# Output product with two of eight pairs of K tiles as seven block products

## The chip, the cores and the metric

The kernel runs on one core of a Trainium2 chip. A core has five engines that run side by side, each its own list of instructions in a fixed order: TensorE (PE in the profile, its weight loads PEld), VectorE (DVE), ScalarE (ACT), GpSimd (POOL) and SyncE (SP, which here issues the transfers). They meet through semaphores. The metric is the device time of one execution in microseconds, lower is better; the time before is the median of three runs.

## The reference

One layer on x of 256 rows by 2048 columns: a SwiGLU feed-forward half step, a mixing step of two head groups with one input projection and one output projection, a second feed-forward half step and a norm. What the change touches is the output projection, the second line here:

```python
y = concatenate([y_rwkv, y_lru], axis=-1)      # 256 x 2048
h = h + y @ w_out[l]                           # w_out: 2048 x 2048
h = h + 0.5 * swiglu(rms_norm(h, ffn2_norm[l]), ...)
```

`y_rwkv` (columns 0 to 1023 of y) comes from a recurrence, `y_lru` (columns 1024 to 2047) from a second recurrence whose result is normed over its 1024 columns: `y_lru = rms_norm(scan * gelu(gate), lru_norm)`.

## The kernel before

All matrix products are made at about float32 precision from two rounded parts of each operand, `hi` and `lo` (`hi` is the operand cast to fp32r, `lo` what is left): a product is three matmuls, hi by hi, hi by lo and lo by hi, that add up in one PSUM bank of 128 by 512.

**The output product** is `mix_out`. It makes two passes (`hf`), one for each half of 1024 columns of w_out. In a pass K runs over 16 tiles of 128 (`NK`), and the 256 rows are two tiles (`t`), the 1024 columns two blocks of 512 (`n`): four banks, each with 3 matmuls for each K tile, so 12 matmuls for a K tile and 192 for a pass. The first pass adds up in banks 0 to 3, the second in banks 4 to 7. Behind each pass DVE adds the banks into `h` (L1099), and `half_done` transposes this half of `h` for the next norm (`transposed`, L228 on PE, L236 on ACT, L237 on DVE), in banks 0 to 3 behind the first pass and 4 to 7 behind the second. K tiles 0 to 7 are `y_rwkv` (tile `xahi_887`, `xalo_888` in the orders below), K tiles 8 to 15 are `y_lru` (`xahi_1042`, `xalo_1043`); both are split by `split_rows` (L1019 on ACT, L1020 on DVE) at the end of `mix_layer`, and the last of these stand while the first pass already runs.

**The weights** come through `weights`: one transfer of 1 MB for two K tiles into `wst` (three buffers), then for each K tile a cast `whi` on ACT (L96) and a difference `wlo` on DVE (L97), 128 by 1024, three buffers each. A transfer starts when the buffer it writes has been split; a cast starts when the matmuls of the K tile three before are through.

**The other scheme is already in the kernel**, in both feed-forward parts: `rows_times_pairs`, with a plan such as `nSnSnSnn`. It takes K tiles in pairs. A pair `n` is 24 matmuls as above. A pair `S` is a 2 by 2 block product by the scheme of Strassen and Winograd: seven products of 128 by 512 instead of eight, 21 matmuls. For it DVE makes four differences of the weight blocks (L136 to L138, in a second buffer of `wst`, called t1 to t4), and these are split as well (three splits of 1024 and one of 512, the last through a tile `whb` of one buffer). The rows need four block sums too, in hi and lo (`block_sums`: four adds of 128 by 128, one cast and one difference of 512). Three of the seven products are shared between outputs: they add up in four banks `aux` beside the four banks `own`, over all S pairs of a pass, and behind the last S pair `shared_h` adds them into `h`.

What sets the order: the program is written in the order of the source, and a scheduler orders each engine's list by priorities and its own estimates when the program is built. On the chip each list then runs in that order.

```python
                self.three(own[0], x(1, 0), w["b21"], first, last)
                self.three(aux[0], x(0, 0), w["b11"], f, l)
                self.three(own[1], sm(4), w["b22"], first, last)
```

In these lines of `rows_times_pairs`, `x` is a block of the rows, `sm` a block sum, and the first three of a pair's seven products are seen.

## Time and profile before

| what | us |
|---|---|
| median of three runs | 1919.07 (1916.38 to 1921.64) |
| the profiled execution, its own time | 1916.57 |
| its span in the trace | 1914.8 |
| PE busy | 1880.0 (98%) |
| DVE busy | 1577.2 (82%) |
| ACT busy | 1033.6 (54%) |
| the output product, first matmul to last | about 1097.3 to 1194.4 |

The span is the time in the trace from the first to the last instruction; 1.8 us of the execution lie around it. A busy engine is one that has an instruction in flight: a matmul of 512 columns is listed with some 390 ns, but the next one starts 227 ns after it. So PE's rate is read from starts, and its idle time from rows that carry a bracket `[idle before <-releaser]`.

### The profile page before, as it was taken

The numbers are of one execution on the slowest core, as the hardware profiler recorded it, in microseconds if no ns is written. First come the engines' busy times: TensorE is split into PE (matmuls) and PEld (weight loads), VectorE is DVE, ScalarE is ACT, GpSimd is POOL, SyncE is SP. The second block draws the span as 40 slices with busy tenths as digits, with TensorE's granted clock in tenths as the row PEclk, the third lists the DMA queues.
The fourth block names the chain that finished last, engine by engine and source line by source line (L and its number), as shares of the span: only waits on it lengthen the run. The fifth ranks groups of instructions, "written<-read, shape, count | busy, mean of one in ns | idle before, by whom it ended". The sixth has DMA issues, their size and how long they took to land.

```text
span 1914.8 us, 25801 instructions
## 1 busy us (share of the span) xinstructions
PE 1880.0 (98%) x10161; PEld 1584.8 (83%) x10161; DVE 1577.2 (82%) x2044; ACT 1033.6 (54%) x1261; POOL 9.7 (1%) x53
## 2 busy tenths in 40 slices
PE   7999999999999999999999999999999999999997
PEld 6888888888888889898899978888888888788886
DVE  7889889898978776976595775989898988987876
ACT  6555555555555555543454554655555555564553
POOL 0000000000000001000000000000000000000000
PEclk9999999999999999998999999999999999999999
DMA  7565555655656556545243456555655655756664
GB/s 238 165 209 180 189 206 184 211 182 207 229 199 228 208 198 212 180 122 152 78 147 116 129 200 204 187 205 184 211 185 204 221 182 176 259 188 203 214 205 141
DMA packets 124402, 360.78 MB, mean 188 GB/s; under 512 B 20879, under 2 KB 23128, under 8 KB 124152
## 3 DMA queue, kind: packets, MB, share of 16 engines
q1 hardware_dynamic: 123960, 358.08, 55.7%
q8 instruction: 79, 1.29, 0.3%
q10 hardware_dynamic: 320, 1.06, 0.1%
q14 instruction: 43, 0.35, 0.1%
HBM read 351.25 MB, written 7.86 MB: 188 GB/s over the span
## 4 chain that ended last, share of the span: by engine, by line
PE 70%; DVE 15%; DMA 11%; issue 2%; ACT 2%; DVEq 0%; SPq 0%; ACTq 0%
PE bank L150 16%; PE bank L149 16%; PE bank L151 16%; DMA wst<-in_ffn_w_gate_dram 6%; DVE wlo L116 6%; DMA wst<-in_ffn_w_up_dram 5%; PE bank L198 3%; PE bank L199 3%; PE bank L200 3%; PE bank L189 2%; PE bank L187 2%; PE bank L186 2%; DVE wlo L97 2%; DVE wst L136 1%; PE bank L768 1%
## 5 line engine op out<-in xcount | busy, mean ns | idle before, releaser
L115 ACT CAST whi<-wst 128x1024 fp32r<-128x1024 f32 (+1 forms) x664 | 652.9, 998 | 585.7 <-PE bank L151 460.8
L116 DVE TENSOR_TENSOR wlo<-wst,whi 128x1024 fp32r<-128x1024 f32 (+1 forms) x664 | 757.5, 1153 | 132.2 <-ACT whi L115 123.5
L97 DVE TENSOR_TENSOR wlo<-wst,whi 128x1024 fp32r<-128x1024 f32 (+2 forms) x153 | 182.7, 1196 | 91.5 <-ACT whi L96 90.8
L96 ACT CAST whi<-wst 128x1024 fp32r<-128x1024 f32 (+2 forms) x153 | 157.6, 1032 | 184.5 <-PE bank L199 103.5
L149 PE MATMUL bank<-whi,hThi 128*128 128x512 f32 x584 | 227.5, 390 | 0.0
L151 PE MATMUL bank<-whi,hTlo 128*128 128x512 f32 x584 | 227.4, 389 | 0.0
L150 PE MATMUL bank<-wlo,hThi 128*128 128x512 f32 x584 | 227.2, 389 | 0.0
L198 PE MATMUL bank<-xahi,whi 128*128 128x256 f32 x688 | 199.8, 291 | 3.7 <-DVE raw L626 3.7
L199 PE MATMUL bank<-xalo,whi 128*128 128x256 f32 x688 | 198.4, 289 | 0.0
L200 PE MATMUL bank<-xahi,wlo 128*128 128x256 f32 x688 | 198.3, 289 | 0.0
L150 PE MATMUL bank<-wlo,xbhi 128*128 128x512 f32 x490 | 191.3, 390 | 1.5 <-DVE wlo L116 1.5
L149 PE MATMUL bank<-whi,xbhi 128*128 128x512 f32 x490 | 191.4, 391 | 0.5 <-DVE hTlo L287 0.5
L149 PE MATMUL bank<-whi,xahi 128*128 128x512 f32 x490 | 191.2, 390 | 0.0
L150 PE MATMUL bank<-wlo,xahi 128*128 128x512 f32 x490 | 190.8, 389 | 0.1
L151 PE MATMUL bank<-whi,xblo 128*128 128x512 f32 x490 | 190.8, 389 | 0.0
L151 PE MATMUL bank<-whi,xalo 128*128 128x512 f32 x490 | 190.7, 389 | 0.0
L198 PEld LDWEIGHTS bank<-xahi,whi 128*128 128x128 f32 x688 | 133.6, 194 | 7.8 <-DVE raw L626 3.9
L136 DVE TENSOR_TENSOR wst<-wst 128x1024 f32<-128x1024 f32 x84 | 102.8, 1224 | 42.6 <-DMA wst<-in_ffn_w_up_dram 16.9
L200 PEld LDWEIGHTS bank<-xahi,wlo 128*128 128x128 f32 x688 | 133.5, 194 | 1.9 <-issue 0.6
L199 PEld LDWEIGHTS bank<-xalo,whi 128*128 128x128 f32 x688 | 133.6, 194 | 1.5 <-issue 0.5
L150 PEld LDWEIGHTS bank<-wlo,hThi 128*128 128x128 f32 x584 | 109.6, 188 | 22.9 <-DVE wlo L116 0.2
L149 PEld LDWEIGHTS bank<-whi,hThi 128*128 128x128 f32 x584 | 109.6, 188 | 22.8
(356 smaller groups left out, 2853.6 us busy)
## 6 DMA issues: line engine op xcount, KB each, us to landing
wst<-in_ffn_w_up_dram SPq DMA_DIRECT2D x88, 1024.0 KB, 5.8
wst<-in_ffn_w_down_dram SPq DMA_DIRECT2D x88, 1024.0 KB, 5.5
wst<-in_ffn_w_gate_dram SPq DMA_DIRECT2D x87, 1024.0 KB, 5.1
wst<-in_w_in_dram SPq DMA_DIRECT2D x40, 1024.0 KB, 5.2
wst<-in_w_out_dram SPq DMA_DIRECT2D x16, 1024.0 KB, 6.4
h<-parked SPq DMA_DIRECT2D x4, 1024.0 KB
wst<-in_w_in_dram SPq DMA_DIRECT2D x4, 640.0 KB, 4.5
h<-in_x_dram SPq DMA_DIRECT2D x4, 512.0 KB
```

The source lines that it names most:

```text
L96: self.last_split = nc.scalar.copy(hi[:, : m * width], src)
L97: nc.vector.tensor_tensor(lo[:, : m * width], src, hi[:, : m * width].bitcast(F32), ALU.subtract)
L115: self.nc.scalar.copy(hv, src)
L116: self.nc.vector.tensor_tensor(lv, src, hv.bitcast(F32), ALU.subtract)
L136: nc.vector.tensor_tensor(t[:, 0:2], b[:, :, 1, :], b[:, 0], ALU.subtract)
L149: nc.tensor.matmul(out, a[0], b[0], start=first, stop=False)
L150: nc.tensor.matmul(out, a[0], b[1], start=False, stop=False)
L151: self.last_mm = nc.tensor.matmul(out, a[1], b[0], start=False, stop=last)
L186: nc.tensor.matmul(banks[t][n][:, :w], a, whi[:, c : c + w], start=first, stop=False)
L198: nc.tensor.matmul(out, a, xhi[:, k, :], start=first, stop=False, skip_group_check=True)
L199: nc.tensor.matmul(out, a, xlo[:, k, :], start=False, stop=False, skip_group_check=True)
L200: nc.tensor.matmul(out, b, xhi[:, k, :], start=False, stop=last, skip_group_check=True)
```

## The change

`mix_out` no longer uses `weights` and `rows_times`, but `rows_times_pairs` with two S pairs in each pass: pairs 4 and 6, that is K tiles 8, 9 and 12, 13, both from `y_lru`. In the first pass the pairs run in the order 0 to 7, so the S pairs are the fifth and the seventh; in the second in the order 0, 1, 4, 2, 6, 3, 5, 7, so they are the third and the fifth. Before the first pass the block sums of pairs 4 and 6 are made (tile `ysums`, from `raw` tiles `ysum`; L1100 is the sum of hi and lo). Both passes use all eight banks. A new pool takes the sums and the scratch tile `osh` of `shared_h`; it lies where `mix_layer` had its tiles.

```diff
-def mix_out(core, w_out, yhi, ylo, after_half):
+def mix_out(core, w_out, yhi, ylo, after_half, pool):
     nc = core.nc
     half = core.D // 2
-    nb = half // 512
+    core.bpool = pool
+    spairs = (4, 6)
+    turns = ((0, 1, 2, 3, 4, 5, 6, 7), (0, 1, 4, 2, 6, 3, 5, 7))
+    sums = pool.tile([P, len(spairs), 2, 512], F32R, name="ysums")
+    for n, p in enumerate(spairs):
+        raw = pool.tile([P, 2, core.S], F32, name=core.name("ysum"), tag="ysum", bufs=2)
+        pair = slice(2 * p, 2 * p + 2)
+        nc.vector.tensor_tensor(raw, yhi[:, pair, :].bitcast(F32), ylo[:, pair, :].bitcast(F32), ALU.add)
+        core.block_sums(raw, sums[:, n, 0, :], sums[:, n, 1, :])
+    of = lambda p: tuple(sums[:, spairs.index(p), i, :] for i in range(2))
     for hf in range(2):
-        db = [[core.bank(4 * hf + t * nb + n) for n in range(nb)] for t in range(core.NT)]
-        for i, (k, hi, lo) in enumerate(core.weights([(w_out, hf * half, half)], list(range(core.NK)))):
-            core.rows_times(db, yhi, ylo, k, hi, lo, half, i == 0, i == core.NK - 1)
+        own, aux = ([core.bank((4 * hf + i) % 8) for i in b] for b in (range(4), range(4, 8)))
+        tmp = lambda: pool.tile([P, 1536], F32, name=core.name("osh"), tag="osh")
+        plan = "".join("nS"[p in spairs] for p in turns[hf])
+        core.rows_times_pairs(w_out, hf * half, plan, turns[hf], own, aux, yhi, ylo, of,
+                              {plan.rindex("S"): [lambda: core.shared_h(aux, tmp(), hf * half, 1.0)]})
         for t in range(core.NT):
-            for n in range(nb):
+            for n in range(2):
                 hs_ = core.h[:, t, hf * half + n * 512 : hf * half + (n + 1) * 512]
-                nc.vector.tensor_tensor(hs_, hs_, db[t][n], ALU.add)
+                nc.vector.tensor_tensor(hs_, hs_, own[2 * t + n], ALU.add)
         after_half(hf)
...
-        mix_out(core, dram["w_out"][0], *xa, half_done)
+        with tc.tile_pool(name="ysums", bufs=1, reuse_waits="tile") as ypool:
+            mix_out(core, dram["w_out"][0], *xa, half_done, ypool)
```

`block_sums` and `shared_h` move from `ffn` into `Core` with the same instructions; `shared_h` gets its scale as an argument. All line numbers behind them shift (L97 becomes L116 in the output product, because it is now `split` that makes the difference; L1020 becomes L1022, L941 becomes L943).

How the lists change, at three places. First DVE's list, some 12 us after the first pass has begun, where the last four tiles of `y_rwkv` are finished (L933 to L941 before). Before:

```order
L97 TENSOR_TENSOR wlo_1553_10070<-wst_1549_10063,whi_1552_10069 128x1024
L937 TENSOR_TENSOR y_1425_9085<-y_1425_9085,bv_1495_9643 128x256
L933 TENSOR_TENSOR y_1425_9085<-y_1425_9085,bank_1497_9650 128x256
L941 TENSOR_TENSOR y_1425_9085<-y_1425_9085,bank_1496_9646 128x256
L936 TENSOR_TENSOR bv_1498_9655<-v_1350_8396,bank_1497_9650 128x256
L97 TENSOR_TENSOR wlo_1556_10100<-wst_1554_10097,whi_1555_10099 128x1024
L937 TENSOR_TENSOR y_1425_9085<-y_1425_9085,bv_1498_9655 128x256
```
And now:

```order
L116 TENSOR_TENSOR wlo_1559_10094<-wst_1555_10087,whi_1558_10093 128x1024
L939 TENSOR_TENSOR y_1425_9085<-y_1425_9085,bv_1495_9643 128x256
L136 TENSOR_TENSOR wst_1566_10157<-wst_1565_10155 128x1024
L943 TENSOR_TENSOR y_1425_9085<-y_1425_9085,bank_1496_9646 128x256
L116 TENSOR_TENSOR wlo_1562_10124<-wst_1560_10121,whi_1561_10123 128x1024
L137 TENSOR_TENSOR wst_1566_10157<-wst_1566_10157,wst_1565_10155 128x512
L935 TENSOR_TENSOR y_1425_9085<-y_1425_9085,bank_1497_9650 128x256
L138 TENSOR_TENSOR wst_1566_10157<-wst_1565_10155,wst_1566_10157 128x512
L938 TENSOR_TENSOR bv_1498_9655<-v_1350_8396,bank_1497_9650 128x256
```
The three differences of the fifth pair's weights (L136 to L138, from the transfer `wst_1565`) have come between the steps that finish y.

Second, where the fifth pair begins. ACT's list from the norm of `y_lru` on (`lss`), before:

```order
L1015 ACT_TABLE_LOAD
L1015 ACTIVATE lss_9009<-lss_9009 128x256
L96 CAST whi_1560_10133<-wst_1559_10131 128x1024
L96 CAST whi_1562_10137<-wst_1559_10131 128x1024
L1019 CAST xahi_1042_5664<-xc_1390_8709 128x256 x3
L96 CAST whi_1565_10167<-wst_1564_10165 128x1024
L1019 CAST xahi_1042_5664<-xc_1390_8709 128x256
L96 CAST whi_1567_10171<-wst_1564_10165 128x1024
```
And now:

```order
L1017 ACT_TABLE_LOAD
L1017 ACTIVATE lss_9009<-lss_9009 128x256
L115 CAST whi_1567_10161<-wst_1565_10155 128x1024
L115 CAST whi_1571_10169<-wst_1566_10157 128x1024
L115 CAST whi_1573_10173<-wst_1566_10157 128x1024
L1021 CAST xahi_1042_5664<-xc_1390_8709 128x256 x4
L115 CAST whi_1576_10200<-wst_1575_10198 128x1024
```
`whi_1567`, `whi_1571` and `whi_1573` are all three `whi` buffers, taken by the S pair (b11 and b21; t1 and t3; t2 and t4), and the casts of y (`xahi`, first K tile 8) now stand behind the third. PE's list a few matmuls into K tile 8, before:

```order
L186 MATMUL bank_1537_9993<-whi_1560_10133,xahi_1042_5664 128x512
L187 MATMUL bank_1537_9993<-wlo_1561_10134,xahi_1042_5664 128x512
L186 MATMUL bank_1538_9994<-whi_1560_10133,xahi_1042_5664 128x512
L187 MATMUL bank_1538_9994<-wlo_1561_10134,xahi_1042_5664 128x512
L189 MATMUL bank_1537_9993<-whi_1560_10133,xalo_1043_5665 128x512
L189 MATMUL bank_1538_9994<-whi_1560_10133,xalo_1043_5665 128x512
L186 MATMUL bank_1535_9991<-whi_1562_10137,xahi_1042_5664 128x512
L187 MATMUL bank_1535_9991<-wlo_1563_10138,xahi_1042_5664 128x512
```
And now, from the seventh matmul of the S pair on:

```order
L151 MATMUL bank_1537_10011<-whi_1567_10161,xalo_1043_5665 128x512
L151 MATMUL bank_1539_10013<-whi_1573_10173,xalo_1043_5665 128x512
L149 MATMUL bank_1537_10011<-whi_1576_10200,xahi_1042_5664 128x512
L149 MATMUL bank_1539_10013<-whi_1576_10200,xahi_1042_5664 128x512
L149 MATMUL bank_1540_10014<-whi_1576_10200,xahi_1042_5664 128x512
L150 MATMUL bank_1537_10011<-wlo_1577_10201,xahi_1042_5664 128x512
L151 MATMUL bank_1537_10011<-whi_1576_10200,xalo_1043_5665 128x512
L150 MATMUL bank_1539_10013<-wlo_1577_10201,xahi_1042_5664 128x512
L151 MATMUL bank_1539_10013<-whi_1576_10200,xalo_1043_5665 128x512
L150 MATMUL bank_1540_10014<-wlo_1577_10201,xahi_1042_5664 128x512
L151 MATMUL bank_1540_10014<-whi_1576_10200,xalo_1043_5665 128x512
L149 MATMUL bank_1538_10012<-whi_1569_10165,ysums_9994 128x512
```
Three products of the S pair are made first, then three of the four banks of the next K tile (`whi_1576`), and in the last row stands the first product that needs a block sum (`ysums`).

Third, DVE's list while y's last tiles are split, before:

```order
L97 TENSOR_TENSOR wlo_1563_10138<-wst_1559_10131,whi_1562_10137 128x1024
L1020 TENSOR_TENSOR xalo_1043_5665<-xc_1390_8709,xahi_1042_5664 128x256 x3
L1084 SCALAR_TENSOR_TENSOR xc_1390_8709<-xc_1390_8709,pc1_5749,lss_9009 128x256
L97 TENSOR_TENSOR wlo_1566_10168<-wst_1564_10165,whi_1565_10167 128x1024
L1020 TENSOR_TENSOR xalo_1043_5665<-xc_1390_8709,xahi_1042_5664 128x256
L1084 SCALAR_TENSOR_TENSOR xc_1485_9571<-xc_1485_9571,pc1_5749,lss_9009 128x256 x4
L97 TENSOR_TENSOR wlo_1568_10172<-wst_1564_10165,whi_1567_10171 128x1024
L1020 TENSOR_TENSOR xalo_1043_5665<-xc_1485_9571,xahi_1042_5664 128x256 x4
L97 TENSOR_TENSOR wlo_1571_10202<-wst_1569_10199,whi_1570_10201 128x1024
```
And now, somewhat later in the list, behind all of these splits of y:

```order
L1100 TENSOR_TENSOR ysum_1536_10003<-xahi_1042_5664,xalo_1043_5665 128x512
L116 TENSOR_TENSOR wlo_1570_10166<-wst_1565_10155,whi_1569_10165 128x512
L246 TENSOR_TENSOR ysum_1535_9995<-ysum_1535_9995 128x128
L136 TENSOR_TENSOR wst_1581_10234<-wst_1580_10232 128x1024
L247 TENSOR_TENSOR ysum_1535_9995<-ysum_1535_9995 128x128
L137 TENSOR_TENSOR wst_1581_10234<-wst_1581_10234,wst_1580_10232 128x512
L248 TENSOR_TENSOR ysum_1535_9995<-ysum_1535_9995 128x128
L138 TENSOR_TENSOR wst_1581_10234<-wst_1580_10232,wst_1581_10234 128x512
L249 TENSOR_TENSOR ysum_1535_9995<-ysum_1535_9995 128x128
L246 TENSOR_TENSOR ysum_1536_10003<-ysum_1536_10003 128x128
L247 TENSOR_TENSOR ysum_1536_10003<-ysum_1536_10003 128x128
L248 TENSOR_TENSOR ysum_1536_10003<-ysum_1536_10003 128x128
```
The block sums of pair 4 (`ysum_1535`, L246 to L249) stand behind the splits of all eight tiles of `y_lru` and take turns with the weight differences of the seventh pair (L136 to L138 on `wst_1580`).

## Rows read from the trace of the kernel before

**Rows 1.** The page, part 1: busy time, share of the span, instructions.

```profile
PE 1880.0 (98%) x10161; PEld 1584.8 (83%) x10161; DVE 1577.2 (82%) x2044; ACT 1033.6 (54%) x1261; POOL 9.7 (1%) x53
```

**Rows 2.** Stretches of the output product: length, busy us of each engine, PEclk, DMA.

```profile
1104.00:1119.40 15.40, 14.34 (x61) 10.62 (x61) 13.19 (x28) 7.29 (x12) 0.00 (x0) 1.00 0.44 137
1119.40:1149.30 29.90, 29.90 (x133) 24.74 (x132) 21.17 (x31) 15.80 (x21) 0.00 (x0) 1.00 0.71 245
1149.30:1194.60 45.30, 45.30 (x209) 37.38 (x208) 25.04 (x29) 19.92 (x24) 0.00 (x0) 1.00 0.65 210
```

**Rows 3.** PE in order of time: start, us, line; twelve matmuls lie between the two.

```profile
1122.11 0.39 PE L186 MATMUL bank<-whi,xahi 128*128 128x512 f32 x1
...
1124.83 0.39 PE L186 MATMUL bank<-whi,xahi 128*128 128x512 f32 x1
```

**Rows 4.** Groups of the whole span: S pairs of the feed-forward, xcount | busy, mean ns | idle before.

```profile
L149 PE MATMUL bank<-whi,xsums 128*128 128x512 f32 x240 | 94.3, 393 | 0.1
...
L136 DVE TENSOR_TENSOR wst<-wst 128x1024 f32<-128x1024 f32 x84 | 102.8, 1224 | 42.6 <-DMA wst<-in_ffn_w_up_dram 16.9 <-DMA wst<-in_ffn_w_down_dram 12.9 <-DMA wst<-in_ffn_w_gate_dram 12.2
L138 DVE TENSOR_TENSOR wst<-wst,wst 128x512 f32<-128x512 f32 x84 | 57.6, 685 | 0.6
```

**Rows 5.** DVE in order of time, from the norm of y_lru on; brackets: idle before.

```profile
1120.70 1.23 DVE L97 TENSOR_TENSOR wlo<-wst,whi 128x1024 fp32r<-128x1024 f32 x1 [0.86 <-ACT whi L96]
1122.43 1.75 DVE L1016 RECIPROCAL lss<-lss 128x256 f32<-128x256 f32 x1 [0.50 <-ACT lss L1015]
1124.10 1.16 DVE L97 TENSOR_TENSOR wlo<-wst,whi 128x1024 fp32r<-128x1024 f32 x1
...
1130.37 1.67 DVE L1084 SCALAR_TENSOR_TENSOR xc<-xc,pc,lss 128x256 f32<-128x256 f32 x4
1131.95 1.22 DVE L97 TENSOR_TENSOR wlo<-wst,whi 128x1024 fp32r<-128x1024 f32 x1
1133.09 1.42 DVE L1020 TENSOR_TENSOR xalo<-xc,xahi 128x256 fp32r<-128x256 f32 x4
1134.43 1.21 DVE L97 TENSOR_TENSOR wlo<-wst,whi 128x1024 fp32r<-128x1024 f32 x1
```

**Rows 6.** ACT in order of time, the same stretch.

```profile
1125.08 1.05 ACT L96 CAST whi<-wst 128x1024 fp32r<-128x1024 f32 x1 [1.68 <-PE bank L189]
1126.04 1.01 ACT L1019 CAST xahi<-xc 128x256 fp32r<-128x256 f32 x3
1127.79 1.06 ACT L96 CAST whi<-wst 128x1024 fp32r<-128x1024 f32 x1 [0.74 <-ACT xahi L1019]
```

**Rows 7.** DVE, two small adds of one block sum in the feed-forward, the second reading the first.

```profile
521.84 0.28 DVE L298 TENSOR_TENSOR hsum<-hsum 128x128 f32<-128x128 f32 x1
522.16 0.29 DVE L299 TENSOR_TENSOR hsum<-hsum 128x128 f32<-128x128 f32 x1
```

**Rows 8.** Transfers of w_out, 1085 to 1175: issue to landing.

```profile
DMA to landing us min/median/max: 5.6/6.4/7.2
```

**Rows 9.** PE around a wait near the start of the kernel, in order of time.

```profile
42.26 0.40 PE L187 MATMUL bank<-wlo,xahi 128*128 128x512 f32 x1
44.68 0.79 PE L189 MATMUL bank<-whi,xalo 128*128 128x512 f32 x2 [2.02 <-DVE xalo L313]
45.27 0.63 PE L186 MATMUL bank<-whi,xahi 128*128 128x512 f32 x1
...
48.65 0.40 PE L189 MATMUL bank<-whi,xalo 128*128 128x512 f32 x1
```

**Rows 10.** Stretches: around that wait, and behind a longer one (PEclk is the third last number).

```profile
46.00:48.00 2.00, 2.00 (x6) 1.51 (x6) 1.84 (x6) 0.00 (x0) 0.00 (x0) 0.50 0.99 393
...
866.00:868.00 2.00, 0.00 (x0) 0.00 (x0) 2.00 (x2) 0.00 (x0) 0.00 (x0) 0.95 0.47 100
868.00:870.00 2.00, 1.20 (x5) 1.20 (x6) 2.00 (x4) 1.22 (x4) 0.00 (x0) 0.50 0.98 198
...
872.00:874.00 2.00, 2.00 (x11) 2.00 (x11) 0.49 (x3) 1.11 (x2) 0.10 (x1) 0.50 0.63 183
```

More of the change, by code (lines that the diff above doesn't have):

```diff
@@ L240, in transposed, with block_sums, shared_h @@
                 self.marks.append((a, b))
+    def block_sums(self, r, hi, lo):
+        nc = self.nc
+        blk = lambda k, t: r[:, k, t * P : (t + 1) * P]
+        nc.vector.tensor_tensor(blk(1, 1), blk(0, 1), blk(1, 1), ALU.add)
+        nc.vector.tensor_tensor(blk(0, 1), blk(0, 0), blk(0, 1), ALU.subtract)
+        nc.vector.tensor_tensor(blk(0, 0), blk(1, 1), blk(0, 0), ALU.subtract)
+        nc.vector.tensor_tensor(blk(1, 0), blk(1, 0), blk(0, 0), ALU.subtract)
+        flat = r.rearrange("p k s -> p (k s)")
+        nc.scalar.copy(hi, flat)
+        nc.vector.tensor_tensor(lo, flat, hi.bitcast(F32), ALU.subtract)
+    def shared_h(self, aux, tmp, c0, scale):
+        nc = self.nc
+        t1, t2, t3 = (tmp[:, i * 512 : i * 512 + 512] for i in range(3))
+        nc.scalar.copy(t1, aux[0])
+        nc.vector.tensor_tensor(t2, aux[2], t1, ALU.add)
+        nc.vector.tensor_tensor(t3, aux[3], t2, ALU.add)
+        for (t, n), parts in (((0, 1), (aux[1], t2)), ((1, 0), (t3,)), ((1, 1), (aux[1], t3)), ((0, 0), (t1,))):
+            hs = self.h[:, t, c0 + n * 512 : c0 + (n + 1) * 512]
+            for part in parts:
+                nc.vector.scalar_tensor_tensor(hs, part, scale, hs, ALU.mult, ALU.add)
     def sumsq(self, c0, w, acc, pool):
@@ L292, in hidden_T @@
                 nc.scalar.copy(raw[:, j // 2].rearrange("p k s -> p (k s)"), bk)
-                block_sums(raw[:, j // 2], *sums(k // 2))
-    def block_sums(r, hi, lo):
-        blk = lambda k, t: r[:, k, t * P : (t + 1) * P]
-        nc.vector.tensor_tensor(blk(1, 1), blk(0, 1), blk(1, 1), ALU.add)
-        nc.vector.tensor_tensor(blk(0, 1), blk(0, 0), blk(0, 1), ALU.subtract)
-        nc.vector.tensor_tensor(blk(0, 0), blk(1, 1), blk(0, 0), ALU.subtract)
-        nc.vector.tensor_tensor(blk(1, 0), blk(1, 0), blk(0, 0), ALU.subtract)
-        flat = r.rearrange("p k s -> p (k s)")
-        nc.scalar.copy(hi, flat)
-        nc.vector.tensor_tensor(lo, flat, hi.bitcast(F32), ALU.subtract)
+                core.block_sums(raw[:, j // 2], *sums(k // 2))
     def normalised(p):
@@ L330, in shared @@
         nc.vector.tensor_tensor(d22, aux[1], d21, ALU.add)
-    def shared_h(aux, tmp, c0):
-        t1, t2, t3, _ = blocks_of(tmp)
-        nc.scalar.copy(t1, aux[0])
-        nc.vector.tensor_tensor(t2, aux[2], t1, ALU.add)
-        nc.vector.tensor_tensor(t3, aux[3], t2, ALU.add)
-        for (t, n), parts in (((0, 1), (aux[1], t2)), ((1, 0), (t3,)), ((1, 1), (aux[1], t3)), ((0, 0), (t1,))):
-            hs = core.h[:, t, c0 + n * 512 : c0 + (n + 1) * 512]
-            for part in parts:
-                nc.vector.scalar_tensor_tensor(hs, part, 0.5, hs, ALU.mult, ALU.add)
     pending = []
@@ L392, in ffn @@
             if i % 2 and i // 2 in place:
-                block_sums(room(i // 2), *sums(place[i // 2]))
+                core.block_sums(room(i // 2), *sums(place[i // 2]))
         for t in range(NT):
@@ L407, in earlier_sums @@
             nc.vector.tensor_tensor(hraw[:, n], hT_hi[:, pair, :].bitcast(F32), hT_lo[:, pair, :].bitcast(F32), ALU.add)
-            block_sums(hraw[:, n], *hsums(p))
+            core.block_sums(hraw[:, n], *hsums(p))
     for piece, (c0, w) in enumerate(down):
@@ L418, in ffn @@
             hooks[DOWN_HIDDEN_AT] = [partial(f, sums=hsums) for f in pending]
-        tmp = lambda: fpool.tile([P, NT, 1024], F32, name=core.name("dsh"), tag="hid")
-        hooks[plan.rindex("S")] = [lambda: shared_h(aux, tmp(), c0)]
+        tmp = lambda: fpool.tile([P, 1536], F32, name=core.name("dsh"), tag="hid")
+        hooks[plan.rindex("S")] = [lambda: core.shared_h(aux, tmp(), c0, 0.5)]
         core.rows_times_pairs(wd, c0, plan, ids, own, aux, hT_hi, hT_lo, hsums, hooks)
```

## The prediction

> **What bounds the kernel now.** I began with the page's busy times [rows 1]: PE has matmuls in flight for 98% of the span, DVE works 82%. That is an average, so I asked for the stretches of the output product [rows 2]. From 1119.4 to 1194.6 PE is busy all of the time, at the granted clock 1.00 (2.4 GHz); DVE works 21.17 of 29.90 us and then 25.04 of 45.30. Only ahead of that, while `y_rwkv` is finished, does PE miss 1.06 of 15.40 us. So TensorE's rate bounds this stage, and the rate is read from starts: twelve matmuls take 1124.83 - 1122.11 = 2.72 us, 0.227 each [rows 3]. The timeline of DVE and ACT shows how near the feeding engines run. ACT's cast of a K tile waits for PE's release of a buffer (1.68 us idle, released by L189 [rows 6]), so weights are ready two to three K tiles ahead and not more. The tiles of `y_lru` come later still: the reciprocal of their norm starts at 1122.43, their last splits at 1133.09 [rows 5]. PE needs K tile 8 at about 1127.55: the two rows of PE are the starts of K tiles 6 and 7, and one more takes 2.72 [rows 3]. Before, it got each tile just ahead of its use.
>
> **What is removed.** Each pass has two S pairs of 21 instead of 24 matmuls: 4 x 3 x 0.227 = 2.7 us less on the bounding engine, 1.4 for each pass. The Trainium skill (TensorE: Matmul & The Clock Gate, section Back-to-back issue gap) has about 131 ns for a matmul of 512 columns in a stream; by it 1.6 us would be saved and my sum be 1.1 us higher. The trace of this kernel has 0.227, and I stay with it.
>
> **What is added on the path, first pass.** Let K be the time at which PE ends K tile 7.
>
> (a) The finish of `y_rwkv`. DVE's list now has L136, L137 and L138 of the fifth pair between these steps: 1.14 + 0.60 + 0.60 = 2.3 us by steps (their 1224 and 684 ns [rows 4] less the overlap of one with the next, as wlo at 1133.09 - 1131.95 = 1.14 [rows 5]). L136 stands ahead of the y step whose bank PE's next gate product needs, so PE waits with it. DVE has idle time of 0.86 + 0.50 us soon after [rows 5], which takes up some of it. Bounds: 0.9 (2.3 less 1.36) and 2.3; I take 1.2, near the lower end, since other small idle times lie ahead. This moves K.
>
> (b) The start of the S pair. The third of its buffers, `whi_1573`, is released by the last matmul of K tile 7, and the casts of y's K tile 8 stand behind this cast in ACT's list. Release to cast is 0.28 us, the cast 1.05 (at 1125.08, where K tile 6 ends at 1124.83) [rows 3, 6], the first cast of y 0.40 (1.01 us for three in steps): PE starts at K + 1.7, where before it went on at K. Wait: 1.7.
>
> (c) The next K tile's cast (`whi_1576`) needs a buffer that PE's eighth S matmul releases at K + 3.55; it ends 1.35 later, at K + 4.9, while PE's nine matmuls ended at K + 3.8. Wait: 1.1. Its `wlo` ends 1.25 us behind the cast, and PE has three matmuls (0.7) to put between: wait 0.65. PE's six other matmuls then end at K + 7.6.
>
> (d) The block sums. DVE's list from there, with steps from rows 5 (a difference of 1024 1.14, of 256 0.34, L1084 0.40, one of 512 0.60): `wlo_1577` ends at K + 6.2; three splits of y 1.0; the last tile's L1084, cast and split 1.2; two sums of hi and lo 1.2; the small weight split 0.6; then up to L249 of pair 4 the four small adds, 4 x 0.2, taking turns with 1.14 + 0.60 + 0.60 for the seventh pair, and 0.1 where one reads the last: 3.2. So K + 13.4. ACT's cast of the sum, 0.65: PE goes on at K + 14.1. Wait: 6.5. Its third matmul needs the lo part, which DVE makes behind that cast and three more small adds: 0.4. Two dependent small adds are 0.32 apart [rows 7], 0.2 if they are not; of this I put 0.1 in.
>
> Sum of (b) to (d): 1.7 + 1.1 + 0.65 + 6.5 + 0.4 = 10.4 us. The bounds: 0 if everything were covered by PE's work, as for the S pairs of the feed-forward, where L149 on sums idles 0.1 us in 240 [rows 4]; there the sums are old when the product begins. Here they are born in it, so the rows of (d) decide. Above, 12.
>
> (e) The last pair's transfer waits for `wlo` of K tile 11, which is late by (d). It lands 5.6 us after its issue (the fastest, since little else loads then) [rows 8], and PE then has some 5 us of work left: wait 0.7. At 6.4 or 7.2 us it is 1.5 to 2.3.
>
> First pass: 1.2 + 10.4 + 0.7 - 1.4 = +10.9.
>
> **Second pass.** Sums are ready. Three things are new. The S pair's first `aux` bank is a bank of the transposes, and DVE reads the last of these (L237) behind the seventh pair's L136, its small split and L137: 1.14 + 0.60 + 0.60, wait 2.2. The K tile behind the S pair gets its `whi` buffer from the matmul just ahead of it: 1.3 for the cast and 0.35 for its `wlo`, as in (c). The fourth pair in the list comes late by 0.35. Together 4.2; before, no wait at all [rows 2]. The bounds are 0 and, with slow transfers, 8. Less 1.4: +2.8. The Trainium skill (Perfetto Trace Analysis, section Matmuls) says that independent groups should rotate through different PSUM banks so that emptying one overlaps the next; with eight banks for each pass this change has none left. By the rows only the first `aux` bank costs, since the pass's four `own` banks are emptied by `shared_h` (some seven steps of 0.60) under the eighth pair's 24 x 0.227 = 5.4 us; if they were not covered, it would be up to 4 us more.
>
> **The clock.** After 2.02 us without a matmul [rows 9] the granted clock was 0.50, the 1.2 GHz level [rows 10]; eight matmuls from 45.27 to 48.65 took 0.42 each instead of 0.227, which is 1.6 us lost. After the longer wait of which 866 to 868 is part, it was 0.50 for 6 us [rows 10], up to 3 us lost at a dense PE. The wait in (d) is 6.5 us: I take 1.6, with 0 and 4 as bounds.
>
> **The sum.** 10.9 + 2.8 + 1.6 = +15.3 us. The feed-forward behind it is bound by PE again and gives nothing back. The profiled execution took 1916.57 us (span 1914.8): 1931.9. The median of the runs is 2.5 above that execution, so the forecast in the measure's terms is 1919.07 + 15.3 = 1934.4.
>
> **The rivals.**
> 1. All is covered, as in the feed-forward [rows 4]. Then only the saving is left: 1919.07 - 2.7 = 1916.4. This is the other side. It decides by one point: whether pair 4's sums are there before PE ends its six matmuls of K tile 10. For it: DVE is idle for 29.90 - 21.17 = 8.7 us of the first stretch and for 20.3 of the second [rows 2]. Against it: the first pass adds some 2 x 4.1 us of weight work (1.14 + 0.60 + 0.60 of differences, 1.14 + 0.60 of splits for a pair), 4 of sums and 4 to 5 of `shared_h`, so DVE has 38 us to do beside 28.5 of PE; and the sums stand behind all eight splits of y, which end at 1134.4 even in the kernel before [rows 5], 7 us after K. Chance 0.07.
> 2. Sums in time, buffers not: only the waits of (a), (b), (c) and half of the second pass's stay: 1.2 + 3.5 + 2 - 2.7 = +4, 1923. For it: each of these waits is for one of three `whi` buffers, which the S pair takes all at once. Chance 0.08.
> 3. The second pass runs without waits: 1934.4 - 4.2 = 1930.2. For it: a transfer or a bank a little earlier is enough. Chance 0.10.
> 4. Transfers land in 7.2 instead of 5.6 us [rows 8]. Five of them are on the path (the fifth and the last pair's in the first pass, three in the second), as S pairs take two of the three `wst` buffers: 5 x 1.6 = 8 more, 1942.4. Chance 0.13.
>
> **How the numbers follow.** The forecast has 0.62, rivals 0.07, 0.08, 0.10 and 0.13. About 0.3% (5.8 us) is what a measurement of this kernel can tell from no change. Slower by more: forecast, rivals 3 and 4: 0.85. Within: rivals 1 and 2, 0.14. Faster by more needs over 5.8 us where 2.7 is all that is removed: 0.01. The range leaves out rivals 1 and 2 and what lies beyond rival 4: 1925 to 1943.
>
> **What would show it.** In the changed profile: 372 matmuls of 512 columns in the product instead of 384; an idle of 5 to 8 us on PE ahead of a matmul on `ysums` in the first pass, released by ACT's cast or by DVE; waits of about 1 to 2 us ahead of it, released by ACT's casts; PEclk 0.50 for some us behind it; the feed-forward behind as long as before. No idle ahead of `ysums` would make me wrong; idle there that a transfer ends, with L136 the one that waits, would be rival 4.

## The result, and the profile after

The changed kernel takes 1934.99 us (median of four runs, 1932.24 to 1938.29) against 1917.97 for the kernel before (four runs, 1916.38 to 1921.64): it is slower by 17.0 us. The ratio on record is 1.0092, interval 1.0078 to 1.0107; the two medians alone give 1.0089. The forecast was 1934.4, or +15.3. The profiled execution took 1932.24 (span 1930.5), 15.7 more than that of before.

The page of the changed kernel, part 1, beside [rows 1]: TensorE (PE) is again busy 98% of the time, with 12 matmuls fewer.

```profile
PE 1883.5 (98%) x10149; PEld 1583.4 (82%) x10149; DVE 1605.2 (83%) x2092; ACT 1042.3 (54%) x1273; POOL 9.6 (0%) x53
```

So the average says nothing. The stretches of the output product do (length, busy us of PE, PEld, DVE, ACT, POOL, then PEclk and DMA), to be read against [rows 2], where PE missed nothing behind 1119.4:

```profile
1105.00:1126.00 21.00, 19.39 (x82) 14.43 (x80) 17.63 (x32) 9.75 (x15) 0.00 (x0) 1.00 0.21 69
1126.00:1146.00 20.00, 11.06 (x35) 7.74 (x36) 16.48 (x35) 8.83 (x16) 0.00 (x0) 0.83 0.47 159
1146.00:1174.00 28.00, 27.94 (x130) 22.39 (x128) 25.23 (x31) 14.86 (x20) 0.00 (x0) 1.00 0.73 245
1174.00:1184.00 10.00, 6.23 (x20) 4.60 (x20) 6.78 (x12) 2.52 (x5) 0.00 (x0) 0.83 0.13 51
1184.00:1210.00 26.00, 25.95 (x113) 20.58 (x112) 19.56 (x22) 12.91 (x13) 0.00 (x0) 1.00 0.72 243
```

There are two holes, one in each pass: 9 us without a matmul in 1126 to 1146, and 3.8 in 1174 to 1184, both in stretches with a granted clock of 0.83. PE in order of time shows what each wait was for (in brackets the idle time and what ended it):

```profile
1108.55 0.70 PE L941 MATMUL bank<-lora_in,g2a 128*128 128x256 f32 x2 [1.12 <-DVE y L943]
...
1127.42 0.50 PE L149 MATMUL bank<-whi,xahi 128*128 128x512 f32 x1 [1.50 <-ACT xahi L1021]
...
1130.72 0.97 PE L149 MATMUL bank<-whi,xahi 128*128 128x512 f32 x3 [0.94 <-ACT whi L115]
1132.04 0.51 PE L150 MATMUL bank<-wlo,xahi 128*128 128x512 f32 x1 [0.35 <-DVE wlo L116]
...
1139.93 0.79 PE L149 MATMUL bank<-whi,ysums 128*128 128x512 f32 x1 [6.23 <-ACT ysums L251]
...
1176.74 0.47 PE L149 MATMUL bank<-whi,xahi 128*128 128x512 f32 x1 [2.59 <-DVE xblo L237]
...
1178.86 2.04 PE L149 MATMUL bank<-whi,xahi 128*128 128x512 f32 x4 [1.18 <-ACT whi L115]
```

The long one is a chain that can be read from DVE and ACT. DVE:

```profile
1133.86 0.43 DVE L1022 TENSOR_TENSOR xalo<-xc,xahi 128x256 fp32r<-128x256 f32 x1 [0.47 <-ACT xahi L1021]
1134.20 1.28 DVE L1100 TENSOR_TENSOR ysum<-xahi,xalo 128x512 f32<-128x512 f32 x2
1135.40 0.68 DVE L116 TENSOR_TENSOR wlo<-wst,whi 128x512 fp32r<-128x512 f32 x1
1136.00 0.28 DVE L246 TENSOR_TENSOR ysum<-ysum 128x128 f32<-128x128 f32 x1
1136.21 1.22 DVE L136 TENSOR_TENSOR wst<-wst 128x1024 f32<-128x1024 f32 x1
...
1138.95 0.28 DVE L249 TENSOR_TENSOR ysum<-ysum 128x128 f32<-128x128 f32 x1
```

and then ACT:

```profile
1139.26 0.62 ACT L251 CAST ysums<-ysum 128x512 fp32r<-128x512 f32 x1 [4.92 <-DVE ysum L249]
```

DVE works without a pause from the last split of y to the last of the four small adds, which take turns with the seventh pair's L136 to L138 at the steps of [rows 4, 5]; PE's last matmul before the hole ends at 1133.5, when the first of the sums has not begun.

From here on one number serves for all kernels: **the product**, from its first matmul to the end of its last (read from starts: the start of the last plus 0.23). Before it was 97.43 us (1097.28 to 1194.71), after it is 115.63 (1094.31 to 1209.94), so +18.2. The whole execution grew by 15.7 only, mostly because the changed kernel came to the product 2.97 us earlier, through a part that the change does not touch. In two later executions of the changed kernel it came there at 1095.02 and 1096.70, so this is scatter and no gain.

### The profile page after: what moved, and what is told of

Its sections match the earlier page's. It is cut to its first block, busy times and chain, and to the rows that moved or that the text cites. A ratio compares the mean times of both kernels' runs of the same rounds, so it can differ in the third digit from the quotient of the medians.

```text
span 1930.5 us, 25840 instructions
## 1 busy us (share of the span) xinstructions
PE 1883.5 (98%) x10149; PEld 1583.4 (82%) x10149; DVE 1605.2 (83%) x2092; ACT 1042.3 (54%) x1273; POOL 9.6 (0%) x53
## 4 chain that ended last, share of the span: by engine, by line
PE 72%; DVE 14%; DMA 10%; ACT 2%; issue 2%; DVEq 0%; ACTq 0%; SPq 0%
PE bank L149 16%; PE bank L151 16%; PE bank L150 16%; DVE wlo L116 6%; DMA wst<-in_ffn_w_gate_dram 6%; PE bank L198 4%; PE bank L199 4%; PE bank L200 4%; DMA wst<-in_ffn_w_up_dram 4%; PE bank L189 2%; PE bank L187 2%; PE bank L186 1%; DVE wst L136 1%; DMA wst<-in_w_out_dram 1%; ACT whi L115 1%
## 5 line engine op out<-in xcount | busy, mean ns | idle before, releaser
L115 ACT CAST whi<-wst 128x1024 fp32r<-128x1024 f32 (+1 forms) x704 | 693.2, 999 | 629.5 <-PE bank L151 484.0
L116 DVE TENSOR_TENSOR wlo<-wst,whi 128x1024 fp32r<-128x1024 f32 (+1 forms) x704 | 803.0, 1153 | 142.6 <-ACT whi L115 134.1
L149 PE MATMUL bank<-whi,xahi 128*128 128x512 f32 x598 | 232.0, 393 | 6.4 <-DVE xblo L237 2.6
L150 PE MATMUL bank<-wlo,xahi 128*128 128x512 f32 x598 | 234.0, 391 | 0.5 <-DVE wlo L116 0.4
L151 PE MATMUL bank<-whi,xalo 128*128 128x512 f32 x598 | 232.4, 391 | 0.0
L96 ACT CAST whi<-wst 128x1024 fp32r<-128x1024 f32 (+2 forms) x121 | 123.9, 1027 | 145.6 <-PE bank L199 101.0
L97 DVE TENSOR_TENSOR wlo<-wst,whi 128x1024 fp32r<-128x1024 f32 (+2 forms) x121 | 143.6, 1189 | 62.3 <-ACT whi L96 61.4
L136 DVE TENSOR_TENSOR wst<-wst 128x1024 f32<-128x1024 f32 x88 | 107.7, 1224 | 48.9 <-DMA wst<-in_ffn_w_up_dram 18.8
L149 PEld LDWEIGHTS bank<-whi,xahi 128*128 128x128 f32 x598 | 112.4, 189 | 32.0 <-ACT whi L115 3.7
L150 PEld LDWEIGHTS bank<-wlo,xahi 128*128 128x128 f32 x598 | 112.6, 188 | 25.4 <-DVE wlo L116 2.2
```

Source lines behind the costliest of these rows:

```text
L96: self.last_split = nc.scalar.copy(hi[:, : m * width], src)
L97: nc.vector.tensor_tensor(lo[:, : m * width], src, hi[:, : m * width].bitcast(F32), ALU.subtract)
L115: self.nc.scalar.copy(hv, src)
L116: self.nc.vector.tensor_tensor(lv, src, hv.bitcast(F32), ALU.subtract)
L136: nc.vector.tensor_tensor(t[:, 0:2], b[:, :, 1, :], b[:, 0], ALU.subtract)
L149: nc.tensor.matmul(out, a[0], b[0], start=first, stop=False)
```

## Experiments

Each time stands beside the kernel before, run on the same chip (1917.51, 1915.20 and 1916.49 us on the three chips).

### S pairs in one pass alone

```diff
-        plan = "".join("nS"[p in spairs] for p in turns[hf])
+        plan = "".join("nS"[p in spairs and hf == 1] for p in turns[hf])
...
```

> S pairs in the second pass alone; the first pass has eight pairs n. In the profile of the changed kernel the second pass shows a wait of 2.75 us on the transposes' bank, 1.35 on a whi buffer, eight matmuls at half clock (1.7 us more) and 0.3 of small stalls, less 1.4 saved: +4.7. Theory (each pass pays its own waits): 1918.0 + 4.7 = 1922.7. Rival A (the second pass is late only because the first leaves VectorE behind with its work, seven steps of shared_h among it): no waits in the second pass, 1916.6. Rival B (the first pass is slowed by the sums' work on VectorE wherever they are used): first pass as slow as now, 1927 or more.

Measured: 1917.30 us, ratio 0.999 (0.9975 to 1.0006), no change that can be measured. The product is 96.09 us (1095.29 to 1191.38), and from 1117 on PE misses nothing and the clock stays:

```profile
1117.00:1191.00 74.00, 74.00 (x336) 61.15 (x335) 62.80 (x90) 40.07 (x52) 0.00 (x0) 1.00 0.68 228
```

My theory fell and rival A holds. The second pass alone costs nothing: it gives back 1.34 us for its six matmuls, 0.223 each, which is the saving to the digit. All of its waits in the changed kernel come out of the first pass. Rival B falls too: the sums are made here as well, and the first pass has the waits of the kernel before (0.65 and 0.39 us) and no more.

The gain does not reach the whole time: in this profiled execution the feed-forward behind the product took 714.1 us, against 708.1 in the kernel before. More on that below.

The other half, with `hf == 0`:

> S pairs in the first pass alone; the second has eight pairs n. Theory: the first pass keeps its waits (1.1 + 1.66 + 1.13 + 0.5 + 6.39) and 2.4 us of half clock less 1.4, about +12 to +13; 1935.0 - 4.7 = 1930.3. Rival A (the second pass is late only through the first): the second pass then gives back nothing but its own saving, and the two singles add up to less than the whole: also near 1930, so here the trace decides, by the idle time ahead of ysums (6 us expected).

Measured: 1930.78 us, ratio 1.0064 (1.0040 to 1.0089), +13.3. The product is 110.37 us, +12.9, with the waits of the first pass to 0.3 us (1.39, 1.50, 0.95, 0.35) and the same hole:

```profile
1142.15 0.79 PE L149 MATMUL bank<-whi,ysums 128*128 128x512 f32 x1 [6.25 <-ACT ysums L251]
```

The singles add up to 12.9 - 1.3 = +11.6, the whole is +18.2: 6.6 us are there only when both passes have S pairs.

### What the long wait is for

```diff
-    sums = pool.tile([P, len(spairs), 2, 512], F32R, name="ysums")
-    for n, p in enumerate(spairs):
...
-    of = lambda p: tuple(sums[:, spairs.index(p), i, :] for i in range(2))
+    old = [v[:, 0:2, :].rearrange("p k s -> p (k s)") for v in (yhi, ylo)]
+    of = lambda p: tuple(old)
```

> The block sums are left out: the S products take the hi and lo parts of K tiles 0 and 1, which are there long before, in place of the sums (so the product is another one); all else stays. Theory (PE waits for the sums at the end of VectorE's list): of the wait of 6.39 us some 1.0 to 1.5 is left, for the small split wlo that stands ahead of the sums; with so short a wait no half clock behind it (2.4 us back): 1935.0 - 5.0 - 2.4 = 1927.6. Rival (the wait is for weights, their splits or transfers, and the sums only stand last by the profile): 1933 to 1935, an idle of 5 us or more at the same place.

Measured: 1927.62 us, ratio 1.0050 (1.0034 to 1.0066), +10.1 where the changed kernel has +17; the time expected, though not all of it from where I expected it. The product is 107.32 us, 8.3 shorter. The hole is gone, and with it the wait of 1.50 for y's first cast, since the S pair now has matmuls on old data to put ahead of it. But waits of 0.57 and 1.13 us are left, and the clock still falls behind them, which I had not expected. (Two more, of 0.61 and 0.76 us at 1150.62 and 1152.57, leave it at 1.00.) PE, then two stretches:

```profile
1138.40 0.73 PE L150 MATMUL bank<-wlo,xahi 128*128 128x512 f32 x2 [0.57 <-DVE wlo L116]
1138.97 0.88 PE L151 MATMUL bank<-whi,xalo 128*128 128x512 f32 x2
1140.98 1.22 PE L149 MATMUL bank<-whi,xahi 128*128 128x512 f32 x2 [1.13 <-ACT whi L115]
```

```profile
1140.00:1142.00 2.00, 1.02 (x2) 0.50 (x2) 1.66 (x3) 2.00 (x4) 0.00 (x0) 0.69 0.00 0
1142.00:1144.00 2.00, 1.96 (x5) 1.48 (x5) 1.12 (x3) 0.24 (x1) 0.00 (x0) 0.50 0.82 276
```

The second pass has a single wait left, 1.02 us, for `shared_h` (DVE h L264); the one on the transposes' bank is gone. More on that below.

A second edit moves the same sums, ahead of the weight work in DVE's list:

```diff
-        nc.vector.tensor_tensor(raw, yhi[:, pair, :].bitcast(F32), ylo[:, pair, :].bitcast(F32), ALU.add)
-        core.block_sums(raw, sums[:, n, 0, :], sums[:, n, 1, :])
+        with core.tc.high_priority(offset=6000):
+            nc.vector.tensor_tensor(raw, yhi[:, pair, :].bitcast(F32), ylo[:, pair, :].bitcast(F32), ALU.add)
+            core.block_sums(raw, sums[:, n, 0, :], sums[:, n, 1, :])
```

> The block sums are put ahead of the weight work in VectorE's list (both L1100, then the eight small adds by turns, then the small weight split and the seventh pair's differences). They still stand behind all splits of y. Theory (PE waits for the end of this list): both L1100 1.2, eight adds of 0.2, the cast 0.65 behind the last split: the sums are there 2.2 us sooner, the wait ahead of ysums 4.0 to 4.5 instead of 6.2, 2 us less in all if no weights come late by it. Rival (what stands behind the sums then comes late in its turn): wait 4 to 4.5, but 1 to 2 us of new waits ahead of the seventh pair, total unchanged.

Measured: 1928.97 us, ratio 1.0064 (1.0051 to 1.0078), beside 1933.77 of the changed kernel on the same chip. The wait is 2.3 us shorter:

```profile
1140.24 0.51 PE L149 MATMUL bank<-whi,ysums 128*128 128x512 f32 x1 [3.90 <-ACT ysums L251]
```

Of that the product keeps 1.0 us (114.57 against 115.60): the bank wait of the second pass is 2.84 us, where the changed kernel has 2.54 on that chip, and most of the rest goes to the half clock behind the second pass's waits, which lasted longer here: the sixteen matmuls from 1179.52 on took 6.41 us, in the changed kernel the sixteen from 1181.41 on 5.19. The other 3.8 us by which the medians differ lie outside the product (in the profiled executions, a feed-forward of 706.2 us against 709.8). So the wait is as short as the theory had it, but neither its 2 us nor the rival's new waits ahead of the seventh pair are there.

### The clock behind the wait

Twenty-four matmuls on old data, into an `aux` bank that the pair then starts anew, stand where PE waits for the sums:

```diff
+                for _ in range(self.fill if f else 0):
+                    yb = [v[:, 0:2, :].rearrange("p k s -> p (k s)") for v in (xhi, xlo)]
+                    y0 = [v[:, 0, 0:P] for v in (xhi, xlo)]
+                    for a, b in ((0, 0), (0, 1), (1, 0)):
+                        self.fills.append(nc.tensor.matmul(aux[2], y0[a], yb[b], start=(a, b) == (0, 0), stop=(a, b) == (1, 0)))
                 self.three(own[1], sm(4), w["b22"], first, last)
```

(`self.fill` is 8 in the first pass and 0 elsewhere; a few more lines order the `fills` behind the matmuls of K tile 10.)

> Work is added: 24 matmuls of 512 columns on old data into a free aux bank (which the product then starts anew), in TensorE's list right behind the six matmuls of K tile 10, where it waits 6.39 us for the sums; 24 x 0.227 = 5.4 us. Theory (the idle time costs twice: the wait, and half clock behind it): the granted clock stays at 1.00, the twelve matmuls on the sums start every 0.227 instead of 0.427 us, 2.4 us back: 1932.6 in spite of the added work. Rival A (the clock falls for another reason): 1935.0. Rival B (the sums would be there before the 5.4 us are over): slower than 1935.0, by up to 5.4.

Measured: 1927.98 us, ratio 1.0051 (1.0038 to 1.0065), +10.5. The product is 113.51 us, 2.1 shorter than the changed kernel's in spite of 5.4 us of added work. In the changed kernel the matmuls on the sums start 0.43 apart:

```profile
1140.53 0.63 PE L150 MATMUL bank<-wlo,ysums 128*128 128x512 f32 x1
1140.95 0.63 PE L151 MATMUL bank<-whi,ysums 128*128 128x512 f32 x1
...
1144.79 0.40 PE L151 MATMUL bank<-whi,ysums 128*128 128x512 f32 x1
```

With the wait filled, they start 0.23 apart from the second on, as in [rows 3]:

```profile
1141.69 0.39 PE L180 MATMUL bank<-xahi,xalo 128*128 128x512 f32 x1
1142.88 0.50 PE L149 MATMUL bank<-whi,ysums 128*128 128x512 f32 x1 [0.81 <-ACT ysums L262]
1143.22 0.39 PE L150 MATMUL bank<-wlo,ysums 128*128 128x512 f32 x1
1143.45 0.40 PE L149 MATMUL bank<-whi,ysums 128*128 128x512 f32 x1
```

And the stretches, of the changed kernel and then of the filled one:

```profile
1142.00:1144.00 2.00, 2.00 (x7) 1.52 (x6) 0.96 (x2) 0.28 (x1) 0.00 (x0) 0.50 0.66 270
```

```profile
1142.00:1144.00 2.00, 1.19 (x6) 0.94 (x6) 1.77 (x6) 0.74 (x2) 0.00 (x0) 1.00 0.37 86
```

So half clock follows the idle time, as in [rows 9, 10], and it costs 2.4 us behind this wait (from 1139.93 to 1145.03 the changed kernel starts twelve matmuls, 5.10 us instead of 2.72). The sums arrive when they did: 1136.47 to 1142.88 is 6.41 us, against 6.39.

The whole time gained more than the product. Two runs were made to see whether that is scatter:

> The run with 24 added matmuls once more, beside the changed kernel on the same chip. In its first run the product was 2.1 to 4.3 us shorter than the changed kernel's, the whole time 6 to 8 us. Theory (only the half clock behind the wait is saved, the rest is scatter of the feed-forward): 2 to 4 us faster than the changed kernel. Rival (it gains in the feed-forward too): 6 to 8 us faster again, no idle of TensorE in the feed-forward.

> The changed kernel beside the run with added matmuls: 1934, product 115.6 to 117.8.

Measured: 1927.32 us for the filled kernel (1.0056, 1.0041 to 1.0071) and 1933.77 for the changed one (1.0084, 1.0067 to 1.0100), 6.5 apart, with products of 115.59 and 115.60. So the rival holds: nearly all of it is gained behind the product, in the feed-forward. From the product's end to the last matmul the filled kernel takes 703.1 and 703.2 us with no idle row at all, the changed one 708.5 and 709.8, the kernel before 708.1. In one stretch of it, the changed kernel and then the filled one, first runs:

```profile
1500.00:1600.00 100.00, 99.26 (x442) 81.06 (x441) 88.69 (x101) 55.59 (x63) 0.00 (x0) 1.00 0.56 197
```

```profile
1500.00:1600.00 100.00, 100.00 (x450) 82.80 (x449) 91.19 (x104) 54.50 (x61) 0.00 (x0) 1.00 0.56 192
```

The lists of all engines are the same there in both, by lines and tile names, and also in the kernel with S pairs in the second pass alone, whose feed-forward took 714.1 us. The length goes with the program, but why one gets along without the small waits on `wlo` stays open: no run tells how matmuls so far ahead should do it.

In this second run the product itself gained nothing. The half clock behind the sums was saved, but the bank wait of the second pass was 0.3 us longer (2.86), and the half clock behind it lasted longer: the sixteen matmuls from 1179.64 on took 6.52 us, against 5.19 in the changed kernel. From 4 to 6 us behind that start, in the filled kernel and then in the changed one on the same chip:

```profile
1183.64:1185.64 2.00, 2.00 (x6) 1.61 (x5) 0.00 (x0) 0.00 (x0) 0.00 (x0) 0.52 0.00 0
```

```profile
1185.41:1187.41 2.00, 2.00 (x10) 1.64 (x10) 0.00 (x0) 1.01 (x2) 0.00 (x0) 1.00 0.00 0
```

The wait just ahead of these matmuls is the same in both (1.18 us, for `whi`); the bank wait before it is not. So a bank wait longer by 0.3 us went with 1.3 us more at half clock, and kernels with such waits whose products differ by a microsecond or two can't be told apart by one execution each.

### Why the second pass waits

> The changed kernel once more, beside the next three: 1935, the product from its first matmul to its last 115.6 us long (97.4 before), with the waits of 1.1, 1.5, 0.9, 0.35, 6.2, 2.6 and 1.2 us. Should its time outside the product differ by some us from the first run, with the product as long, that part is scatter of this kernel's feed-forward and not the change's.

Measured: 1933.96 us, ratio 1.0093 (1.0078 to 1.0108), product 117.77: the waits of the first pass to 0.15 us, the bank wait 3.34 instead of 2.59, and behind it the longer half clock too (sixteen matmuls in 6.56 us, in the first run 5.34). The next two have their edits in the second and in the first pass:

```diff
-    turns = ((0, 1, 2, 3, 4, 5, 6, 7), (0, 1, 4, 2, 6, 3, 5, 7))
+    turns = ((0, 1, 2, 3, 4, 5, 6, 7), (0, 1, 2, 3, 4, 5, 6, 7))
```

> The changed kernel, with the pairs of the second pass in the order 0 to 7, so that its S pairs are the fifth and the seventh and not the third and the fifth. Theory (the second pass waits because VectorE comes out of the late first pass with a backlog, which it has worked off a few pairs later): no waits in the second pass, product 2.75 + 1.35 + 1.7 + 0.3 = 6.1 us shorter than the changed kernel's, 109.5; time near 1929. Rival (the S pairs of the second pass wait for buffers and banks of their own, wherever they stand): waits of 1 to 3 us at the fifth pair, 113 or more; time 1933 to 1935.

Measured: 1928.76 us, ratio 1.0065 (1.0049 to 1.0082), +13.6 against +18.8 of the changed kernel on the same chip. The product is 109.76 us (expected 109.5); in the second pass 0.43 us of waits are left, on `wlo`, where the changed kernel on that chip has 3.34 and 1.18. Two pairs later the S pairs find everything ready.

```diff
-                              {plan.rindex("S"): [lambda: core.shared_h(aux, tmp(), hf * half, 1.0)]})
+                              {plan.rindex("S"): [lambda: core.shared_h(aux, tmp(), hf * half, 1.0)] if hf else []})
```

> Left out: the addition of the shared products of the first pass into h (shared_h, one copy and eight operations of VectorE of 0.60 us), so the first half of h lacks them; all else stays. Theory A (this work is the backlog that makes the second pass wait): no waits in the second pass, product 109.5, time near 1929. Theory B (the backlog is the weight work that the late first pass has pushed together): the wait of 2.6 us stays at 1.5 or more, product 113 or more, time 1932 to 1935.

Measured: 1924.51 us, ratio 1.0042 (1.0027 to 1.0056), +9.3. The product is 109.44 us (expected 109.5), the first pass has the same hole (6.24), and in the second PE misses next to nothing:

```profile
1150.00:1205.00 55.00, 54.81 (x249) 44.81 (x248) 44.26 (x54) 28.82 (x34) 0.00 (x0) 1.00 0.73 246
```

Theory A holds: without `shared_h` there is no wait. How, DVE tells. In the changed kernel the bank wait is ended by the second of these two rows, with the fifth pair's weights between them:

```profile
1172.87 0.48 DVE L237 SCALAR_TENSOR_TENSOR xblo<-bank,gT,xbhi 128x256 fp32r<-128x256 f32 x1
1173.77 1.23 DVE L136 TENSOR_TENSOR wst<-wst 128x1024 f32<-128x1024 f32 x1 [0.43 <-DMA wst<-in_w_out_dram]
...
1176.12 0.48 DVE L237 SCALAR_TENSOR_TENSOR xblo<-bank,gT,xbhi 128x256 fp32r<-128x256 f32 x1
```

The first L237 stands 78.6 us behind the product's first matmul. Without `shared_h` it comes at 70.8 (1166.54 - 1095.70), with equal first passes up to the sums:

```profile
1166.54 0.47 DVE L237 SCALAR_TENSOR_TENSOR xblo<-bank,gT,xbhi 128x256 fp32r<-128x256 f32 x1
```

That is 7.8 us sooner, more than the eight operations of 0.60 themselves: what stood behind them also comes in another order (the fifth pair's L136 and L137 now ahead of the first L237). And `shared_h` does not do it alone. In the kernel without block sums it is still made, but the first pass has no hole (and DVE no sums to make); there the first L237 comes 71.7 us behind the product's first matmul, and no matmul waits for the transposes' bank:

```profile
1168.06 0.48 DVE L237 SCALAR_TENSOR_TENSOR xblo<-bank,gT,xbhi 128x256 fp32r<-128x256 f32 x1
```

So by these runs the wait on that bank takes both: a first pass that ends late, with `shared_h` behind it. Not tried was `shared_h` behind a first pass that is on time, or the same work later in DVE's list.

Last, a first pass that should have avoided the late sums, with pair 6 alone as S pair, the seventh:

```diff
-        plan = "".join("nS"[p in spairs] for p in turns[hf])
+        plan = "".join("nS"[p in spairs[1 - hf :]] for p in turns[hf])
```

> In the first pass pair 6 alone is an S pair, as the seventh; the second pass as changed, with two S pairs as the third and fifth. Theory (what costs is that sums are born later than the product that uses them, and the first pass ends late by it): the sums are there by the seventh pair, no idle of more than 1 us ahead of ysums, half clock nowhere, 3 x 3 x 0.227 = 2.0 us saved: product 95.4 to 96.5, time 1915.5 to 1916.6. Rival (shared_h behind the first pass is enough to make the second pass wait, as in the changed kernel): the second pass costs its 6.1 us, product 101.5, time 1921.6.

Measured: 1929.20 us, ratio 1.0070 (1.0053 to 1.0087), +14.0; the product is 108.46 us. Both fell, the theory by far and the rival by 7 us. The sums are late even for the seventh pair (both pairs' sums were still made, by turns, behind all splits), and the second pass waits again, first for `shared_h` itself. Two smaller waits are not shown, 0.76 us for `wlo` ahead of the sums and 0.62 for L237; the clock fell to 0.50 twice, behind the first and the third of these:

```profile
1145.28 0.51 PE L149 MATMUL bank<-whi,ysums 128*128 128x512 f32 x1 [2.74 <-ACT ysums L251]
...
1160.34 0.50 PE L149 MATMUL bank<-whi,xahi 128*128 128x512 f32 x1 [0.73 <-DVE h L264]
...
1175.74 0.50 PE L150 MATMUL bank<-wlo,xahi 128*128 128x512 f32 x1 [2.25 <-DVE wlo L116]
```

### A version that could be faster

Since S pairs in the second pass alone cost nothing, that pass was given three, with the first pass as in the kernel before:

```diff
-    spairs = (4, 6)
-    turns = ((0, 1, 2, 3, 4, 5, 6, 7), (0, 1, 4, 2, 6, 3, 5, 7))
+    spairs = (4, 5, 6)
+    turns = ((0, 1, 2, 3, 4, 5, 6, 7), (0, 1, 4, 2, 5, 3, 6, 7))
...
-        plan = "".join("nS"[p in spairs] for p in turns[hf])
...
+        plan = "".join("nS"[hf == 1 and p in spairs] for p in turns[hf])
...
```

> The first pass as in the kernel before, eight pairs n; in the second pass three S pairs (4, 5 and 6) as the third, fifth and seventh. Theory (a second pass that starts on time has room for them): no waits, 3 x 3 x 0.227 = 2.0 us saved, product 95.4; time 2.0 us under the kernel before, 0.1%, less than a measurement can tell, so the trace decides. Rival (three are more than VectorE and the buffers can feed): waits of 0.4 to 1.5 us at the seventh pair, product 96 to 99.

Measured: 1918.30 us, ratio 1.0007 (0.9998 to 1.0017): no change. The product is 97.76 us, longer than before by 0.3; waits for `wlo` of 0.40, 0.15 and 0.67 us have eaten the saving of 2.0, as the rival had it, though at the sixth and the eighth pair and not at the seventh. (Read from starts they cost 2.1 us: the matmuls that waited start 0.79, 0.54 and 1.07 us behind the one before instead of 0.23, and the next one each time 0.1 late.) The feed-forward took 713.0 us here, again longer than before. The longest of the waits:

```profile
1189.91 0.50 PE L150 MATMUL bank<-wlo,xahi 128*128 128x512 f32 x1 [0.67 <-DVE wlo L116]
```

No version here beats the kernel before by more than can be measured.

## Why the prediction was right, and where it was not

The time and the range held. That the time was met to 0.6 us is luck: the median before was taken as 1919.07 and is 1917.97 with the fourth run, and the growth was forecast at 15.3 us, where 17.0 were measured here and 18.8 and 17.3 in two more comparisons. The product itself grew by 18.2, 2.9 more than the sum, and the profiled execution came near the forecast only because it reached the product 2.97 us earlier.

Of the steps these held, with what the starts on PE give for the changed kernel:

- **Saved, 2.7.** The second pass alone gives 1.34 for six matmuls, so 2.7 for twelve. The Trainium skill (TensorE: Matmul & The Clock Gate, section Back-to-back issue gap) has some 131 ns for a matmul of 512 columns in a stream; the saving in the run with the second pass alone is 223 for each.
- **(a) 1.2**: 1.12 + 0.20 + 0.20 less the 0.41 that PE waited for y's cast before: 1.1.
- **(b) 1.7**: from the end of K tile 7's last matmul (1125.53 + 0.23) to 1127.42, 1.7. **(c) 1.1 and 0.65**: 1.13 and 0.51. (By its own terms, 1.25 less 0.7, the second should have been 0.55. In (b), [rows 3, 6] give 0.25 from release to cast and not 0.28; neither changes the sum by more than 0.1.)
- **(d) 6.5**: 6.39. The 0.4 for the lo part did not show, since the matmuls ahead of it ran at half clock.

The first step that failed is **(e)**, 0.7 for the last pair's transfer: no such wait here, and in the other runs with the same first pass at most 0.24 us, for the eighth pair's first cast. The second is the **clock**, 1.6, taken for one wait. It fell twice, to 0.50 behind the sums and again in the second pass, and cost 2.4 and some 1.7 (from 1178.86 to 1182.38 PE starts eight matmuls, 3.5 us instead of 1.8). That is just beyond my upper bound of 4, and in the next run of the changed kernel the second one was longer still.

The third is the step that matters. For the **second pass** I summed 2.2, 1.3 and twice 0.35; the trace shows 2.75, 1.35 and some 0.3. The sizes are right, and so is the order on DVE (L237 behind L136, the small split and L137). The reason is not. I had these as the price of an S pair where it stands, "the S pair's first `aux` bank is a bank of the transposes", and of `shared_h` I said that the eighth pair's 5.4 us cover it. The runs show otherwise: S pairs at the same places wait for nothing when the first pass has none, and the waits go when `shared_h` is left out, or when the S pairs come two pairs later; the wait on the transposes' bank also goes when the first pass has no hole. It is not PE that `shared_h` holds up in the changed kernel but DVE's own list, where the emptying of the transposes' banks and the weight splits stand behind it. In the two kernels with other first passes PE even waits for it directly (1.02 and 0.73 us, DVE h L264). The Trainium skill (Perfetto Trace Analysis, section Matmuls) has independent groups rotate through banks so that emptying one overlaps the next; here the same eight banks do without a wait once DVE is on time, so the lack of banks is not enough for the wait.

The terms as measured, 1.1 + 1.7 + 1.6 + 6.4 in the first pass, 2.4 + 1.7 for the clock, 2.75 + 1.35 + 0.3 in the second, less 2.7, make +16.6 of the product's +18.2. The rest lies in many small steps that I did not take apart. One kind of them: behind a wait the next matmul starts late too, as at 1127.42, where it follows 0.33 us later instead of 0.23.

Of the rivals, 3 (a second pass without waits) is what happens as soon as `shared_h` is not ahead of it. Rival 4 had L136 wait for a transfer ahead of the sums; the L136 shown above has no bracket, so DVE did not wait there. Rival 1 is right for the second pass alone and has the reason for it: sums that are old when their product begins. That the feed-forward is as long as before holds for the changed kernel (708.1 before, 708.3 to 709.8 after) and not for each of the experiments, whose feed-forwards took from 703.1 to 714.1 us. That range of 11 us is as large as many of the effects here, so the products are to be compared, and not the whole times alone.

## What to carry over

A scheme that trades TensorE's matmuls for work of VectorE wants inputs that are old. Here, where they were (the second pass alone), it took 1.34 us off the product, too little to be measured in the whole; in the first pass, whose operands were still being finished, it saved 1.4 us of matmuls and the product grew by 12.9. Price the work that ends such a stage (here `shared_h`) not only by whether the matmuls wait for it, but by what stands behind it in its engine's list, in the next stage too, above all when the stage ends late. And run each half alone before costing the halves separately: here the second cost nothing by itself and over 6 us behind the first.
